# Hybrid encoder layer on one core: side work moved one step apart from what it feeds, and the bias rows made first

## The chip, the cores and the metric

The kernel runs on one core of a Trainium2 chip. The metric is the device time of one execution in microseconds (us), and lower is better. A run here is one timed execution; the kernel before was run three times. One further execution was recorded by the hardware profiler, and all rows below are from that one.

The engines are named as in the profile: PE is the matrix engine (PEld its weight loads), DVE the vector engine, ACT the scalar engine, POOL the general engine, SP the engine that issues most transfers. Each engine works through its own instructions strictly in order, and so does each queue of transfers.

## The reference, cut to what matters

```python
def trunk(x, p, ...):                          # the same weights for 512 + 256 tokens
    proj = rmsnorm(x, norm_g) @ w_in            # 2048 -> 12288
    s_x, s_z, q, k, v, a_z, g_s, g_a = split(proj)
    y = s5(s_x, forward) + s5(s_x, backward) + d * s_x       # state-space scan, 64 groups of 64 states
    y = gelu(y); y = y * sigmoid(y @ glu_w + glu_b); y_s = (y * silu(s_z)) @ w_branch_s
    for h in range(4):                           # difference attention
        s = q[h, c] @ k[h, c].T / sqrt(128) + bias[h]        # c = 0, 1
        w = softmax(s[0]) - lam * softmax(s[1])
        o[h] = w @ v[h]
    y_a = (rmsnorm(o) * 0.2 * silu(a_z)) @ w_branch_a
    x = x + (sigmoid(g_s) * y_s + sigmoid(g_a) * y_a) @ w_out
    x = x + sigmoid(rmsnorm(x, ple_g) @ ple_gate_w) * (p @ ple_proj_w)
    return rmsnorm(x, final_g)
```

## The kernel before, in words

All 768 tokens are held together, features on partitions (128 at a time). The large products with the weights are the main line of the program. Each float32 weight is split into a rounded part (`wh`, made by ACT) and a rest (`wl`, made by DVE), and each product is done as three products of 128x128 by 384 columns. A list of blocks is worked through in order; a block has pieces of 1024 weight columns, and a piece has four products of 12 matmuls. A `Quad` block (it forms q, k and the gates) has seven such products, and DVE and ACT form sums and splits of weights for the next Quad between them.

Everything else runs in lanes beside the main line. A lane is a Python generator. Before a product of the main line, `slot_e` lets each lane write its work for DVE, ACT, POOL and SP up to its next `yield`; after the product, `slot_p` lets it write its work for PE. Two yields are one step. `pace` sets how many steps there are to a product (0.7 early on, `PACE[0..2]` in the state-space part, 0.9 and 1.0 in the attention). So a lane decides by its yields how many products of the main line lie between two of its pieces of work, and if the work that PE needs in a step is not ready when PE comes to it, PE stands still, the main line too.

Four lanes matter here.

- `s5_params` loads the parameters of the state-space part and a one-hot table (`p_oh`, `p_rb`), computes powers of the complex decay (`p_pw`) by a long row of small DVE instructions, and has ACT copy them into tables `tw` and `tq`. After that it makes the four bias rows of the attention: for each head two matmuls into two banks (`bb`), two ACT copies to `bo`, one transfer to `d_bias`. Heads 0 and 2 use banks 4 and 5, heads 1 and 3 banks 6 and 7.
- `s5_half`, run for two halves of the groups, ends with a loop over 8 batches `b`: ACT and DVE copy states into `sb`, SP loads a table `tp` (8 transfers), inputs `u` and a table `q`, and PE forms `yps` from them; ACT copies `yps` to `Y` one turn later, and every second turn 8 transfers write `Y` to `d_yr`. A turn is two steps.
- `att_prep(h)` loads v, k and q of a head from memory (`d_v`, `d_k`, `d_qq`) into one buffer `raw`, scales them and splits each into two parts. The next head's preparation starts before a head is done.
- `att_head(h)` works on six query blocks, one every four steps. `plan_e` and `plan_p` say in which step of a block each function runs: `scores` (PE), `soft1` (DVE: adds the bias, maximum), `expo` (ACT), `soft2` (DVE: the difference of the two softmaxes, in `p`), `wt_pe` (PE: transposes `p` into bank 6, `wt`), `wt_split` (ACT, DVE), `pv` (PE: `o`), `osq`, `ors`, `ors2`, `ocopy` (square, POOL power, scale), `ot_pe` (PE: `ot`, bank 4, which `scores` uses too), `ot_out` (ACT).

The blocks of the gated unit (`ev_glu`: sigmoids on ACT) follow the last Quad. Their inputs `y` are loaded and split (`y_load`, `y_split`) in the last two products of that Quad.

Of the kernel before, what the change touches and what calls it, by code (L numbers as in the profile page):

```python
# [18 lines left out]
EPS = 1e-6  # L19
G = 64  # L20
FB = 11
PACE = 0.9, 0.85, 1.0
IDLE, MPS, ID2 = 5, 2, 2
CONSTS = (("ident", 128), ("norm_g", 16), ("mask16", 16), ("ssm_d", 8), ("final_g", 16), ("glu_b", 8), ("subg", 2),
          ("ple_g", 16), ("lamv", 4))
# [31 lines left out]
def _build(tc, nc, d, es, dbg):  # L57
# [37 lines left out]
    def bank(i, name):  # L95
        return ps.tile([128, 512], F32, tag=f"b{i}", name=name)
# [15 lines left out]
    def later(fn, n=1):  # L112
        pend.append((slot[0] + n, fn))
# [611 lines left out]
    def s5_params(sp):  # L725
# [15 lines left out]
        yield  # L741
        yield

        def dve_exp(out, x):
            xc, n, r, p, m = (t_(k + out.tensor.name) for k in ("xc", "en", "er", "ep", "em"))
            ts(xc, x, -87.0, 88.0, ALU.max, ALU.min)
            ts(n, xc, 1.4426950408889634, 12582912.0, M, A_)
            ts(n, n, -12582912.0, None, A_)
            stt(r, n, -0.693359375, xc, M, A_)
            stt(r, n, 2.12194440e-4, r, M, A_)  # L750
            cs = [1.9875691500e-4, 1.3981999507e-3, 8.3334519073e-3, 4.1665795894e-2,
                  1.6666665459e-1, 5.0000001201e-1]
            ts(p, r, cs[0], cs[1], M, A_)
            for c in cs[2:]:
                tt(p, p, r, M)
                ts(p, p, c, None, A_)
            tt(p, p, r, M)
            tt(p, p, r, M)
            tt(p, p, r, A_)
            ts(p, p, 1.0, None, A_)  # L760
            ts(n, n, 12582912.0 + 127.0, None, A_)
            e = t_("ee" + out.tensor.name, F, I32)
            nc.vector.tensor_scalar(out=e, in0=n.bitcast(I32), scalar1=23, scalar2=None, op0=ALU.logical_shift_left)
            tt(out, p, e.bitcast(F32), M)
            ts(m, x, -87.0, None, ALU.is_ge)
            tt(out, out, m, M)
# [86 lines left out]
        s5c.update(kr=kr, ki=ki, a8r=a8r, a8i=a8i, tw=tw, tq=tq)  # L853
        yield
        yield

        for h in range(4):
            bb = [bank(4, "bb"), bank(5, "bb")] if h % 2 == 0 else [bank(6, "bb"), bank(7, "bb")]
            yield
            for i in range(2):  # L860
                mm(bb[i], rb[:, h], oh[:, i * 512:(i + 1) * 512], True, True)
            yield
            o = pp.tile([128, 1024], F32, tag="bo", name="bo", bufs=2)
            for i in range(2):
                act(o[:, i * 512:(i + 1) * 512], bb[i])
            later(lambda h=h, o=o: dma(dbias[h], o))
        yield
        yield
        yield
# [3 lines left out]
    def s5_half(hf, sp):  # L873
# [205 lines left out]
        for m in range(1, 64):  # L1079
            if m < 32:  # L1080
                S2 = St.rearrange("p (q m) x g -> p q m x g", q=3)[:, 0:3:2]
                prev, cur = S2[:, :, m - 1], S2[:, :, m]
                sh = [128, 2, 2, 32]
                t1 = op.tile(sh, F32, tag="s1", name="s1")
                t2 = op.tile(sh, F32, tag="s2", name="s2")
                tt(t1, prev, a8r.unsqueeze(1).to_broadcast(sh), M)
                tt(t2, prev[:, :, ::-1], a8i.unsqueeze(1).to_broadcast(sh), M)
                f = lambda a: a.rearrange("p q x g -> p q (x g)")
                tt(f(t1), f(t1), f(cur), A_)
                tt(f(cur), f(t1), f(t2), A_)  # L1090
            else:
                prev, cur = St[:, m - 1], St[:, m]
                sh = [128, 2, 32]
                t1 = op.tile(sh, F32, tag="s1", name="s1")
                t2 = op.tile(sh, F32, tag="s2", name="s2")
                tt(t1, prev, a8r, M)
                tt(t2, prev[:, ::-1], a8i, M)
                tt(t1, t1, cur, A_)
                tt(cur, t1, t2, A_)
            if m % 2 == 0:  # L1100
                if m == 44:
                    load_t(0)
                    load_u(0)
                if m == 48:
                    load_q(0)
                if m == 52:
                    load_q(1)
                yield
                yield
# [6 lines left out]
        for b in range(NB + 1):  # L1116
# [11 lines left out]
            if b < NB:  # L1128
# [5 lines left out]
                        act(sb[0:64, :, x, c0:c0 + n], v[0:64])  # L1134
                        nc.vector.tensor_copy(out=sb[64:128, :, x, c0:c0 + n], in_=v[64:128, :, ::-1])
                load_t(b + 1)
                load_u(b + 1)
            yield
            if b < NB:

# [10 lines left out]
                                mm(o, q[:, j - 1, g], sb[:, g, j - 1], False, j == 2)  # L1151
                prevy = (b, yps)
                load_q(b + 2)
            yield
            yield
            yield
        yield
        yield
# [118 lines left out]
    def att_prep(h):  # L1277
# [22 lines left out]
        for n, src, to in (("k", dk, kk), ("q", dqq, qq)):  # L1300
            rw = atile("raw", (128, 2, T), F32)
            for c in range(2):
                dma(rw[:, c], src[(2 * h + c) * 128:(2 * h + c + 1) * 128, :])
            yield
            yield
            yield
            yield
            for c in range(2):
                if n == "q":
                    stt(rw[:, c], rw[:, c], 128.0 ** -0.5, R, M, M)  # L1310
# [15 lines left out]
    def att_head(h, tb, vh, vl, kk, qq):  # L1326
# [98 lines left out]
            later(lambda: dma(dst, ot))  # L1425


        plan_e = {0: soft1, 1: expo, 2: soft2, 3: wt_split, 5: osq, 6: ors, 7: ors2, 8: ocopy, 10: ot_out}
        plan_p = {-1: scores, 2: wt_pe, 4: pv, 9: ot_pe}
        for m in range(-1, 4 * NT + 8):  # L1430
            if m == 4 * NT - 2 and h < 3:
                lane2.add(att_prep(h + 1))
            for plan in (plan_e, plan_p):
                for k in sorted(plan, reverse=True):
                    if (m - k) % 4 == 0 and 0 <= (m - k) // 4 < NT:
                        plan[k]((m - k) // 4)
                yield
# [529 lines left out]
```

## Time and profile before

| | us |
|---|---|
| median of 3 runs | 2511.86 (2506.81 to 2514.24) |
| the profiled execution | 2505.9 |
| its span, first to last instruction | 2504.1 |
| PE busy in the span | 2396.3 (96%) |
| DVE, ACT, POOL busy | 1385.2, 974.1, 149.8 |

The span leaves 1.8 us of the profiled execution outside. A matmul counts as busy until its last column has left the array, and the next has begun by then, so PE's busy time is little more than a statement that PE has work. The time when it is not busy is 108 us, and a part of the busy time is at the lower of PE's two clocks (1.2 GHz in place of 2.4).

### The profile page before, as it was taken

What the parts mean: (1) busy time and instruction counts of PE and PEld (TensorE: products, weight loads), DVE (VectorE), ACT (ScalarE), POOL (GpSimd) and SP (SyncE); (2) the same over time, 40 slices, a digit from 0 to 9 for tenths busy, and PEclk for the clock granted to TensorE, in tenths of its full rate; (3) what the DMA queues carried; (4) which work ended last, traced back from release to release, by engine and by line L of the source; (5) the groups of instructions that cost most, each with busy time, mean ns of one, the idle gap of its engine ahead of it and who ended that gap; (6) DMA issues with size and microseconds to landing.
All of it is one profiled execution on the core that took longest, in us unless ns stands there. A gap on an engine that the chain in (4) does not pass through costs nothing.

```text
span 2504.1 us, 36458 instructions
## 1 busy us (share of the span) xinstructions
PE 2396.3 (96%) x14398; PEld 2354.9 (94%) x14398; DVE 1385.2 (55%) x2569; ACT 974.1 (39%) x1718; POOL 149.8 (6%) x150
## 2 busy tenths in 40 slices
PE   7899999999989999999999899899999999999996
PEld 7799998999989999999898888899999999999986
DVE  8556672566616777654656566557365322253346
ACT  5323213342235555453455555643233211143233
POOL 5000000000000000000111111000000000000003
PEclk9999999999999999999999999999999999999998
DMA  7343235332455677565756557544333222222234
GB/s 293 92 122 116 92 109 165 117 124 100 130 160 152 208 236 210 163 217 133 178 126 149 137 126 176 156 156 164 118 104 112 86 91 78 93 85 87 85 113 163
DMA packets 146347, 345.62 MB, mean 138 GB/s; under 512 B 33600, under 2 KB 55872, under 8 KB 146176
## 3 DMA queue, kind: packets, MB, share of 16 engines
q1 hardware_dynamic: 132352, 306.06, 37.5%
q0 software_dynamic: 13248, 36.18, 9.1%
q8 instruction: 113, 1.85, 0.3%
q10 hardware_dynamic: 576, 1.05, 0.1%
q14 instruction: 58, 0.48, 0.1%
HBM read 238.96 MB, written 104.27 MB: 137 GB/s over the span
## 4 chain that ended last, share of the span: by engine, by line
PE 60%; DVE 3%; ACT 3%; DMA 3%; issue 2%; POOL 1%; SPq 0%; ACTq 0%; DVEq 0%; POOLq 0%
PE acc L93 57%; PE o L93 1%; PE s L93 1%; ACT wh L79 1%; DVE wl L82 1%; POOL y L1649 1%; DMA raw<-d_k 1%; DMA d_az<-stg 1%; PE wt L1379 0%; SPq L99 0%; DVE a L82 0%; DVE p L90 0%; ACT a L79 0%; ACT stg L79 0%; ACT L79 0%
## 5 line engine op out<-in xcount | busy, mean ns | idle before, releaser
L93 PE MATMUL acc<-a,wh 128*128 128x384 f32 (+2 forms) x6072 | 1355.5, 337 | 7.8 <-ACT stg L79 6.2
L93 PEld LDWEIGHTS acc<-a,wh 128*128 128x128 f32 x6072 | 1087.8, 190 | 15.0 <-ACT stg L79 6.5
L93 PE MATMUL acc<-a,wl 128*128 128x384 f32 (+2 forms) x3288 | 878.7, 340 | 16.0 <-DVE wl L82 6.5
L82 DVE TENSOR_TENSOR wl<-raw,wh 128x1024 fp32r<-128x1024 f32 (+1 forms) x279 | 344.9, 1236 | 523.3 <-ACT wh L79 515.2
L93 PEld LDWEIGHTS acc<-a,wl 128*128 128x128 f32 x3288 | 597.4, 190 | 25.8 <-DVE wl L82 6.7
L79 ACT ACTIVATE wh<-raw 128x1024 fp32r<-128x1024 f32 (+1 forms) x321 | 319.6, 996 | 398.9 <-PE acc L93 283.7
L79 ACT ACTIVATE stg<-acc 128x384 f32<-128x384 f32 x312 | 149.2, 489 | 341.0 <-PE acc L93 311.6
L93 PE MATMUL acc<-y,wh 128*128 128x384 f32 (+2 forms) x1024 | 221.8, 335 | 0.0
L93 PEld LDWEIGHTS acc<-y,wh 128*128 128x128 f32 x1024 | 181.0, 188 | 1.8
L93 PE MATMUL acc<-wh,a 128*128 128x256 f32 x768 | 140.3, 285 | 0.0
L93 PE MATMUL acc<-y,wl 128*128 128x384 f32 (+2 forms) x512 | 133.6, 336 | 0.0
L93 PEld LDWEIGHTS acc<-wh,a 128*128 128x128 f32 x768 | 120.9, 194 | 0.0
L93 PE MATMUL acc<-wl,a 128*128 128x256 f32 x384 | 110.6, 288 | 1.8 <-DVE stg L86 1.8
L79 ACT ACTIVATE stg<-stg 128x768 f32<-128x768 f32 (+3 forms) x64 | 43.2, 686 | 173.1 <-DVE stg L82 173.1
L93 PE MATMUL acc<-a,wa 128*128 128x384 f32 x504 | 94.7, 335 | 1.0 <-ACT stg L79 1.0
L79 ACT ACTIVATE stg<-y 128x384 f32<-128x384 f32 (+2 forms) x64 | 32.0, 526 | 160.2 <-DVE y L82 160.2
L93 PEld LDWEIGHTS acc<-y,wl 128*128 128x128 f32 x512 | 92.9, 188 | 0.9
L93 PEld LDWEIGHTS acc<-a,wa 128*128 128x128 f32 x504 | 87.6, 188 | 1.5 <-ACT stg L79 1.4
L93 PEld LDWEIGHTS acc<-wl,a 128*128 128x128 f32 x384 | 74.3, 194 | 2.0 <-DVE stg L86 2.0
L82 DVE TENSOR_TENSOR stg<-acc,R 128x384 f32<-128x384 f32 (+2 forms) x48 | 29.4, 660 | 72.2 <-PE acc L93 72.2
L82 DVE TENSOR_TENSOR y<-acc,stg 128x384 f32<-128x384 f32 x32 | 16.3, 552 | 86.8 <-PE acc L93 86.8
L82 DVE TENSOR_TENSOR raw<-raw,raw 128x512 f32<-128x512 f32 x84 | 58.0, 691 | 2.3
(253 smaller groups left out, 2266.3 us busy)
## 6 DMA issues: line engine op xcount, KB each, us to landing
raw<-in_w_in SPq DMA_DIRECT2D x144, 512.0 KB, 4.2
raw<-in_ple_g_w SPq DMA_DIRECT2D x42, 512.0 KB, 3.6
raw<-in_w_out SPq DMA_DIRECT2D x32, 512.0 KB, 3.6
d_gs<-stg POOLq DMA_DIRECT2D x28, 384.0 KB, 5.9
d_ga<-stg POOLq DMA_DIRECT2D x28, 384.0 KB, 5.4
stg<-in_xT SPq DMA_DIRECT2D x26, 384.0 KB, 4.2
d_q<-q SPq DMA_DIRECT2D x16, 512.0 KB, 3.6
raw<-in_w_v SPq DMA_DIRECT2D x16, 512.0 KB, 4.1
```

The source lines that it names most:

```text
L79: return nc.scalar.activation(out=out, in_=in_, func=func, **kw)
L82: return nc.vector.tensor_tensor(out=out, in0=a, in1=b, op=op)
L93: return nc.tensor.matmul(out, lhsT, rhs, start=start, stop=stop, **kw)
L1649: (nc.gpsimd if b % 3 else nc.vector).tensor_tensor(out=h, in0=h, in1=rb, op=M)
```

## The change

Six edits, all of them in lanes; the main line is the same, product for product.

1. The loop that makes the bias rows stands at the beginning of `s5_params`, before the row of DVE instructions, and no longer after the tables.
2. In the last loop of `s5_half` the two yields that stood behind the products stand between the copies of the states and the products. The turn is still two steps.
3. In the same loop the inputs `u` are loaded two batches ahead and no longer one; `u(1)` is loaded before the loop.
4. In `att_prep` there are six yields between the load of k (and of q) and its first use, where there were four.
5. In `plan_e` and `plan_p` everything from `wt_pe` on is one step later, so that there is one more step between `soft2` and `wt_pe`. The next head's preparation starts one step later.
6. `PACE[1]`, for the scan, is 0.82 and no longer 0.85.

```diff
-PACE = 0.9, 0.85, 1.0
+PACE = 0.9, 0.82, 1.0
...
         yield
         yield
 
+
+        for h in range(4):
+            bb = [bank(4, "bb"), bank(5, "bb")] if h % 2 == 0 else [bank(6, "bb"), bank(7, "bb")]
+            yield
+            for i in range(2):
+                mm(bb[i], rb[:, h], oh[:, i * 512:(i + 1) * 512], True, True)
+            yield
+            o = pp.tile([128, 1024], F32, tag="bo", name="bo", bufs=2)
+            for i in range(2):
+                act(o[:, i * 512:(i + 1) * 512], bb[i])
+            later(lambda h=h, o=o: dma(dbias[h], o))
         def dve_exp(out, x):
...
         s5c.update(kr=kr, ki=ki, a8r=a8r, a8i=a8i, tw=tw, tq=tq)
         yield
         yield
-
-        for h in range(4):
...
-            later(lambda h=h, o=o: dma(dbias[h], o))
         yield
...
                 if m == 44:
                     load_t(0)
                     load_u(0)
+                    load_u(1)
...
                 load_t(b + 1)
-                load_u(b + 1)
+                load_u(b + 2)
+            yield
+            yield
             yield
             if b < NB:
...
                 load_q(b + 2)
             yield
-            yield
-            yield
         yield
...
-            yield
-            yield
-            yield
-            yield
+            for _ in range(6):
+                yield
             for c in range(2):
                 if n == "q":
...
-        plan_e = {0: soft1, 1: expo, 2: soft2, 3: wt_split, 5: osq, 6: ors, 7: ors2, 8: ocopy, 10: ot_out}
-        plan_p = {-1: scores, 2: wt_pe, 4: pv, 9: ot_pe}
+        plan_e = {0: soft1, 1: expo, 2: soft2, 4: wt_split, 6: osq, 7: ors, 8: ors2, 9: ocopy, 11: ot_out}
+        plan_p = {-1: scores, 3: wt_pe, 5: pv, 10: ot_pe}
         for m in range(-1, 4 * NT + 8):
-            if m == 4 * NT - 2 and h < 3:
+            if m == 4 * NT - 1 and h < 3:
                 lane2.add(att_prep(h + 1))
```

Three places show what this does to the order on the engines. The first is ACT near the beginning, in `s5_params`. Before, the copies `bo` of the bias rows stand behind the copies `tw` and `tq` of the tables (`p_sn` and `p_hs` are sines, `wh` the splits of the main line's weights):

```order
L79 ACTIVATE wh_872<-raw_641 128x1024
L79 ACT_TABLE_LOAD
L79 ACTIVATE p_sn<-p_r 128x64
L79 ACTIVATE p_hs<-p_rh 128x64
L79 ACTIVATE wh_992<-raw_724 128x1024
L79 ACTIVATE tw<-p_pw 64x512 x2
L79 ACTIVATE tq<-p_pw 64x512 x2
L79 ACTIVATE tw<-p_pw 64x512 x2
L79 ACTIVATE tq<-p_pw 64x512 x2
L79 ACTIVATE wh_1096<-raw_870 128x1024
L79 ACTIVATE bo<-bb 128x512 x6
L79 ACTIVATE wh_1178<-raw_990 128x1024
```

After the change the same stretch of ACT, from the split of the same piece of weights (`raw_641`) on, is this:

```order
L79 ACTIVATE bo<-bb 128x512 x2
L79 ACTIVATE wh_819<-raw_641 128x1024
L79 ACTIVATE bo<-bb 128x512 x6
L79 ACTIVATE wh_932<-raw_724 128x1024
L79 ACT_TABLE_LOAD
L79 ACTIVATE p_sn<-p_r 128x64
L79 ACTIVATE p_hs<-p_rh 128x64
L79 ACTIVATE wh_1068<-raw_817 128x1024
L79 ACTIVATE tw<-p_pw 64x512 x2
L79 ACTIVATE tq<-p_pw 64x512 x2
L79 ACTIVATE tw<-p_pw 64x512 x2
L79 ACTIVATE tq<-p_pw 64x512 x2
```

The bias copies have moved ahead of the sines and tables, and the tables one piece of weights (four products) further back.

The second place is SP in the last loop of `s5_half`, one turn and the beginning of the next. Before:

```order
L99 DMA tp<-d_z 16x4x128 x8
L99 DMA u<-d_sx 128x384
L99 DMA q<-d_q 128x1024
L99 DMA d_yr<-y 16x8x96 x8
L99 DMA tp<-d_z 16x4x128 x8
```

After:

```order
L99 DMA tp<-d_z 16x4x128 x8
L99 DMA u<-d_sx 128x384
L99 DMA d_yr<-y 16x8x96 x8
L99 DMA q<-d_q 128x1024
L99 DMA tp<-d_z 16x4x128 x8
```

The `u` there is now that of one batch later, and the 8 writes of `Y` stand before the load of `q`, which waits for the products of the turn.

The third place is DVE in a query block of the second head: `soft2` (`r`, `s`, `p`), and the next block of rows up to `wtl`, which needs PE's transposes of that `p`. Before:

```order
L1370 RECIPROCAL r<-su 128x2
L90 SCALAR_TENSOR_TENSOR s_13284<-r,nlam,su 128x1
L90 SCALAR_TENSOR_TENSOR p<-p,s_13284 128x512
L82 TENSOR_TENSOR wl<-raw_13126,wh 128x1024
L82 TENSOR_TENSOR ors<-ors,r 128x1
L82 TENSOR_TENSOR wtl<-wt,wth 128x512
```

After:

```order
L1369 RECIPROCAL r<-su 128x2
L90 SCALAR_TENSOR_TENSOR s_13371<-r,nlam,su 128x1
L90 SCALAR_TENSOR_TENSOR p<-p,s_13371 128x512
L82 TENSOR_TENSOR wa<-raw_13259,wa 128x512
L82 TENSOR_TENSOR raw_13259<-raw_13259 128x512
L87 TENSOR_SCALAR rsm<-oss 128x1
L82 TENSOR_TENSOR raw_13259<-raw_13259,raw_13152 128x512
L82 TENSOR_TENSOR raw_13152<-raw_13152,raw_13259 128x512
L82 TENSOR_TENSOR ors<-ors,r 128x1
L82 TENSOR_TENSOR wtl<-wt,wth 128x512
```

One more product's worth of the main line's splits and sums lies between the difference and what follows its transposes.

Two more facts of the order. The lane of the attention ends 14 products of the main line later than before, so that the last head lies wholly beside the blocks of the gated unit, whose sigmoids need another function table on ACT than the exponentials; ACT has 18 table loads in place of 12. And the last head's q (2 transfers) now stands on SP right before the 8 loads of `y`.

## Rows read from the trace of the kernel before

**Rows 1.** The page: span, and busy time, share and instructions of PE.

```profile
span 2504.1 us, 36458 instructions
PE 2396.3 (96%) x14398; PEld 2354.9 (94%) x14398; DVE 1385.2 (55%) x2569; ACT 974.1 (39%) x1718; POOL 149.8 (6%) x150
```

**Rows 2.** Windows: start:end, length, each engine's busy time (instructions), granted clock, DMA share, GB/s.

```profile
375.00:445.00 70.00, 64.19 (x463) 62.78 (x462) 19.15 (x52) 25.18 (x58) 0.00 (x0) 1.00 0.56 160
665.00:742.00 77.00, 68.63 (x456) 67.06 (x456) 20.09 (x63) 26.02 (x61) 0.00 (x0) 1.00 0.56 159
1190.00:1600.00 410.00, 367.94 (x2100) 356.63 (x2099) 248.39 (x460) 216.01 (x443) 64.62 (x80) 0.95 0.65 150
```

**Rows 3.** Waits of PE, whole span: what waited, releaser, us in total, times, longest.

```profile
PE wt L1379 <- DVE p L90: 26.8, 16, 7.4
PE acc L93 <- ACT stg L79: 11.3, 5, 6.2
PE bb L93 <- ACT bo L79: 7.7, 1, 7.7
...
PE yps L93 <- DVE sb L1135: 4.1, 5, 1.4
...
PE yps L93 <- DMA u<-d_sx: 3.4, 3, 2.0
PE s L93 <- DVE ql L82: 2.9, 1, 2.9
```

**Rows 4.** Timeline, tables and bias rows: start, us, instruction [idle before, releaser].

```profile
105.85 2.25 ACT L79 ACTIVATE tw<-p_pw 64x512 f32<-64x512 f32 x2 [13.83 <-DVE p_pw L82]
...
114.57 1.06 ACT L79 ACTIVATE wh<-raw 128x1024 fp32r<-128x1024 f32 x1
...
116.17 3.77 PE L93 MATMUL bb<-p_oh,p_rb 32*128 32x512 f32 x4 [7.66 <-ACT bo L79]
```

**Rows 5.** Windows on the stretches at half clock: the first; the sum of seven in attention.

```profile
113.18:123.42 10.24, 7.25 (x15) 4.71 (x16) 1.23 (x1) 5.55 (x9) 0.00 (x0) 0.50 0.55 205
...
sum 37.54, PE 29.23 PEld 28.88 DVE 24.75 ACT 16.47 POOL 5.24; mean PE 4.18 PEld 4.13 DVE 3.54 ACT 2.35 POOL 0.75
```

**Rows 6.** Timeline, two turns of the last state-space loop.

```profile
384.64 0.55 ACT L79 ACTIVATE y<-yps 128x192 f32<-128x192 f32 x2 [2.89 <-PE yps L93]
385.09 1.85 ACT L79 ACTIVATE sb<-st 64x256 f32<-64x256 f32 x4
385.24 3.71 SPq L99 DMA_DIRECT2D tp<-d_z  x8
...
397.90 1.10 PE L93 MATMUL yps<-sb,q 128*128 128x96 f32 x8 [1.40 <-DVE sb L1135]
```

**Rows 7.** Timeline, one query block of the second head.

```profile
1385.69 0.47 ACT L79 ACTIVATE on<-o,r 128x256 f32<-128x256 f32 x1 [0.94 <-PE o L93]
...
1391.80 0.63 PE L1379 MATMUL wt<-consts,p 128*128 128x128 f32 x4 [1.73 <-DVE p L90]
```

**Rows 8.** Timeline, preparation of the third head.

```profile
1433.36 1.91 DVE L82 TENSOR_TENSOR raw<-raw,R 128x768 f32<-128x768 f32 x2 [4.66 <-DMA raw<-d_k]
...
1441.72 4.21 PE L93 MATMUL acc<-a,wh 128*128 128x384 f32 x12 [6.22 <-ACT stg L79]
```

**Rows 9.** Timeline, end of the last Quad and loads of `y`.

```profile
1577.92 2.25 PE L93 MATMUL acc<-a,wl 128*128 128x384 f32 x12
1584.39 0.84 ACT L79 ACTIVATE a<-a 128x768 fp32r<-128x768 f32 x1 [1.93 <-DMA a<-d_y]
...
1587.55 1.08 PE L1379 MATMUL wt<-consts,p 128*128 128x128 f32 x4 [7.38 <-DVE p L90]
```

**Rows 10.** Timeline, transposed output `ot` and its copy, second head.

```profile
1387.58 0.38 PE L1418 MATMUL ot<-consts,on 128*128 128x128 f32 x2
1389.11 0.62 ACT L79 ACTIVATE ot<-ot,subg 128x128 f32<-128x128 f32 x2
```

**Rows 11.** Groups of ACT: table loads, count, busy us, mean ns of one, idle before.

```profile
L79 ACT ACT_TABLE_LOAD x12 | 15.4, 1283 | 2.2 <-issue 1.3 <-PEq L1957 0.7
```

More of the change, by code (lines that the diff above doesn't have):

```diff
@@ L855, in s5_params @@
         yield
-        for h in range(4):
-            bb = [bank(4, "bb"), bank(5, "bb")] if h % 2 == 0 else [bank(6, "bb"), bank(7, "bb")]
-            yield
-            for i in range(2):
-                mm(bb[i], rb[:, h], oh[:, i * 512:(i + 1) * 512], True, True)
-            yield
-            o = pp.tile([128, 1024], F32, tag="bo", name="bo", bufs=2)
-            for i in range(2):
-                act(o[:, i * 512:(i + 1) * 512], bb[i])
-            later(lambda h=h, o=o: dma(dbias[h], o))
         yield
@@ L1303, in att_prep @@
                 dma(rw[:, c], src[(2 * h + c) * 128:(2 * h + c + 1) * 128, :])
-            yield
-            yield
-            yield
-            yield
+            for _ in range(6):
+                yield
             for c in range(2):
```

## Prediction

> **What bounds the kernel now.** I read the page first. PE is busy for 2396.3 of 2504.1 us [rows 1]: the main line fills the span, and lanes cost time only where PE stands still for them, or where they cost it its clock. What can be won is therefore in PE's idle 108 us and in the stretches at half clock, and a lane's own length costs nothing as long as some of the main line is left beside it. Next I read the waits of PE over the whole span [rows 3]. The largest by far is the transposes' wait for `soft2` on DVE: 26.8 us in 16 pieces, the longest 7.4. Then come the main line's wait for an ACT copy (11.3), the bias rows' wait for ACT (7.7, one piece), several kinds of wait before the `yps` products, and one wait of the first scores (2.9). Windows show where they lie [rows 2]. In the two last loops of the state-space part PE is idle for 70.00 - 64.19 = 5.8 and 77.00 - 68.63 = 8.4 us, 14.2 together. In the 410 us of attention beside the Quads it is idle for 42 us, and the granted clock is 0.95. DVE is busy there for 248 and ACT for 216 of 410 us, so neither is short of time; what PE waits for is lateness in single steps. Last I looked at the stretches at half clock one by one [rows 5]. All seven of the attention's follow on a standstill of PE. In them PE is busy for 29.23 us, work that takes 14.6 us at full clock: 14.6 us lost on top of the idle time.
>
> A step of the lanes is worth one product of the main line where the pace is 1.0. Twelve matmuls show 2.25 us, the last one's tail included [rows 9]; 2.1 us is what I use.
>
> **Bias rows first.** Before, the third bias group needs banks 4 and 5 emptied by `bo`, and these copies stand behind the tables: ACT waits 13.83 us for DVE's powers, then copies from 105.85 to 114.57, 8.7 us, and only then comes to a split and to `bo` [rows 4]. PE loses 7.66 us and after it runs 7.25 us at half clock, another 3.6 [rows 5]. After the change the groups wait for nothing: the one-hot table has been loaded two steps earlier, and ACT has no long wait ahead of `bo`. The late thing is now the tables. They move back by four steps, at pace 0.7 some 3.0 us each, 12 us, and by up to 16 if DVE, now without its powers to do, first waits for the evacuation of a block. So ACT's 8.7 us end between 126.6 and 130.6, and the split behind them (1.06, and about as much again for its rest on DVE) is ready between 129 and 133. PE, without its standstill, is back from the bias group at 108.5 and has two such groups (4 us before or after) and nine products (19 us) to do until it needs that split, at 131. I take a wait of 2 us that takes the place of 7.7, and half of the slow clock: 5.7 + 1.8 = 7.5 us won. Bounds: nothing (a new wait as long as the old one), and 11.3.
>
> **The last loop of the state-space part.** Copies and products had one product of the main line between them, now they have two. The copies cannot start earlier than before in one respect: ACT's `y` copies, which stand ahead, wait for the products of the turn before, and these now lie in the step just before. From there ACT needs 0.55 + 1.85 = 2.4 us [rows 6] against 4.2, and with a split of 1.06, every second turn, 3.5; that is covered. DVE's copies were late by 1.4 behind a split [rows 6]; one more product covers that. `u` loaded two ahead ends the waits for it (3.4). SP needs 3.71 us for `tp` [rows 6], about as much for the writes of `Y` every second turn, and two single transfers, some 6.4 a turn; PE's turn is 4.2 plus 24 small products, which at the row's 1.10 for eight make 3.3 at most. SP just keeps up, and `tp` keeps its four steps. I let 2 of the 14.2 us stand: 12.2 won. Bounds: 3.4 (only `u`), and 14.2. The pace 0.82 puts a little more than one product more beside each scan, at no cost, since the main line goes on for long after.
>
> **The step after `soft2`.** Without the longest, 15 waits make 19.4 us, 1.3 each; 1.73 is one of them [rows 7]. A step of 2.1 us covers nearly all; 1 us stays. In addition `expo` stood behind the square `on` on ACT, which waits for PE's `o` (0.94 there [rows 7]); that square now runs one step after `expo`, which makes the chain shorter. The longest wait, 7.38 us, is another thing: `soft2` stood on DVE behind the splits of `y`, and ACT's fourth split waited for its transfer until 1584.39 [rows 9]. PE was through with the Quad at about 1580 and needs these very splits next. So the transposes no longer wait there, but the gated unit's first product does. With the last head's q now ahead of `y` on SP, this may even last longer. I leave 5 us. Won: 26.8 - 1 - 5 = 20.8. Bounds: 13 (7.4 stays and a third of the rest returns), and 25.
>
> **Loads of k and q.** DVE stood 4.66 us for k's transfer, and PE 6.22 us in consequence, through ACT's copy of a product's bank [rows 8]. One more step takes 2.1 from that and leaves 4.1; the other main-line waits of the kind (the rest of 11.3, all but half a us) and the scores' 2.9 shrink to some 0.8 together. Won: 14.2 - 4.9, about 9. Bounds: 4 and 13. The later end of the attention costs nothing: its lane is followed by one that has some 28 steps' worth of main line left and needs 24.
>
> **Clock.** Fewer and shorter standstills give back part of the 14.6 us; I keep 6 for those left at `y` and at one preparation: 8.6 won. Bounds: 3 and 12.
>
> **What is added.** The copy of `ot` out of bank 4 now has one product, not two, before `scores` wants the bank. In the tightest block the transposes end at 1387.96 and the copy at 1389.73 [rows 10], where one product more ends at 1389.9: 0.2 us to spare. I charge 2 us over the 12 places. Six more table loads are 6 x 1.28 = 7.7 us of ACT [rows 11]. They lie before `expo`, which has the new step as cover, and before the sigmoids, which two free pairs of banks cover; so nothing on PE's path. Without that cover they cost 7.7. The Trainium skill, ScalarE: Activation LUTs, section "What ACT_TABLE_LOAD costs", counts a drain with each load, about 2.66 us a switch, and its rules say to do all of one set before switching, which speaks against moving the whole last head beside sigmoids. By it the six would be 16 us of ACT. The trace shows 1283 ns a load and only 2.2 us idle ahead of all twelve [rows 11], so the trace's price is the one used. Last, a wait that goes lets the next late thing show. For that I charge a quarter of the step's and the loads' gain, 7.5 us.
>
> **Sum.** 7.5 + 12.2 + 20.8 + 9 + 8.6 = 58.1, less 2 and 7.5: 48.6. The profiled execution was 2505.9, so 2457.3. The three runs lie 0.9 to 8.3 us above that execution; I add 3 and forecast **2460 us**.
>
> **Rivals.**
> *Half of it returns.* In attention PE goes faster and DVE and ACT must keep up; three quarters of the 38.4 us (step, loads, clock) come back as waits of the main line for splits and bank copies. For it: these queues are in order, and one late landing moves everything behind it [rows 8]. Against it: both engines are idle for 40% of that stretch [rows 2]. 7.5 + 12.2 + 9.6 - 2 = 27.3, with the 3 added 2482. Chance 0.18.
> *ACT paces the last head.* All six table loads fall on PE's path: 7.7 more, 2468. For it: `expo` and the sigmoids alternate four steps apart. Against it: the cover above. Chance 0.08. [...]
> *The change does not do what it says.* Each wait moves one step along with what was moved: the tables hold up the main line for 7 us, `y` copies hold back `sb` by a us in each of 16 turns, the attention's waits return in full. 2500 to 2512, chance 0.07. Against it: two of the three need the engines to be full.
> *Slower.* `scores` behind `ot`: where ACT is late, PE waits in the 12 places in which the bank is wanted one step later. It decides from 48.6/12 = 4 us of lateness each; at 5 us it is 60 lost, 2520. For it: a spare of 0.2 us [rows 10], and ACT was once over 6 us late [rows 8]. Against it: that was one transfer in 410 us. Chance 0.05.
>
> **Chances and range.** The forecast has 0.62, with 2445 to 2472 as its own range. Low end: nothing of the 9.5 us charged comes, and a few us of what I left standing go too. The high end of the whole reaches past the first rival, to 2490; outside lie the last two rivals and a little on the low side. About 0.3%, 7.5 us, is what a measurement of this kernel can tell from no change. Faster by more than that: 0.62 + 0.18 + 0.08 = 0.88; within: 0.07; slower: 0.05.
>
> **What would show it.** Right: no wait of `bb` for `bo`; PE's waits before `yps` under 4 us together; `wt` waits for `soft2` under 3 us; a wait of the main line of about 5 us for splits of `y` at the end of the last Quad; a smaller one at one preparation; half-clock stretches in attention under half of 37.5 us; 18 table loads of 1.28 us. The forecast is wrong if PE waits for `ot`, if waits of `acc` for ACT or DVE grow by more than 15 us, or if the split behind the tables holds PE for 5 us or more.

## The result and the profile after

The changed kernel takes 2445.70 us, median of 4 runs (2443.91 to 2450.41), beside 2509.34 (2506.47 to 2514.24, 4 runs) for the kernel before: a ratio of 0.9747, 95% interval 0.9725 to 0.9770, a gain of 63.6 us. The forecast was 2460 us with 2445 to 2490 as its range: the sign and the places were right, the gain was 15 us larger than the sum of 48.6, and the time lies 0.7 us above the low end of the range. The profiled execution is the shortest of the four and has a span of 2442.2 us; its granted clock, as a share of the full 2.4 GHz over the whole span, was 0.992, and the four had 0.992, 0.989, 0.990 and 0.992. The kernel before had 0.985 in its profiled execution.

The page of the changed kernel, which answers to [rows 1]:

```profile
span 2442.2 us, 36464 instructions
PE 2379.0 (97%) x14398; PEld 2341.8 (96%) x14398; DVE 1384.6 (57%) x2569; ACT 980.0 (40%) x1724; POOL 151.9 (6%) x150
```

PE does the same 14398 matmuls. It is idle for 2442.2 - 2379.0 = 63.2 us, where it was 107.8: 44.6 of the 61.9 us of span. Another 17.3 us went from its busy time. Stretches at half clock account for most of them: PE was busy in these for 53.8 us before and is for 23.1 us now, and half of the difference, 15.4 us, is time won. The sums of all windows at half clock, before and after:

```profile
sum 78.75, PE 53.85 PEld 50.94 DVE 44.43 ACT 28.67 POOL 12.25; mean PE 3.85 PEld 3.64 DVE 3.17 ACT 2.05 POOL 0.88
```

```profile
sum 40.18, PE 23.07 PEld 21.10 DVE 25.36 ACT 17.56 POOL 9.73; mean PE 3.85 PEld 3.52 DVE 4.23 ACT 2.93 POOL 1.62
```

PE's waits in the changed kernel, whole span (what waited, releaser, us in total, times, longest), against [rows 3]:

```profile
PE wt L1378 <- DVE p L90: 6.5, 1, 6.5
PE acc L93 <- ACT a L79: 5.5, 5, 2.2
PE acc L93 <- ACT stg L79: 5.1, 6, 1.6
PE yps L93 <- DMA tp<-d_z: 2.8, 2, 1.4
...
PE yps L93 <- DMA d_yr<-y: 1.9, 1, 1.9
...
PE o L93 <- ACT on L79: 0.6, 1, 0.6
PE yps L93 <- issue: 0.6, 1, 0.6
```

The 16 waits of `wt` (26.8 us) have become one. The waits of `bb` for `bo` and of `s` for `ql` have no row any more, and those before `yps` are down to 2.8 + 1.9 + 0.6 = 5.3 us, but for another cause: SP's queue and the landing of `tp`.

Windows of the changed kernel over the same parts of the program (start:end, length, busy time of each engine, granted clock, DMA share, GB/s), against [rows 2]:

```profile
375.00:445.00 70.00, 65.40 (x445) 64.20 (x445) 18.18 (x45) 24.96 (x58) 0.00 (x0) 1.00 0.64 181
665.00:742.00 77.00, 75.61 (x505) 75.19 (x505) 19.98 (x47) 33.94 (x72) 0.00 (x0) 1.00 0.66 202
1180.00:1580.00 400.00, 385.67 (x2259) 375.14 (x2258) 259.00 (x485) 234.71 (x474) 65.55 (x80) 0.98 0.68 163
```

In the attention beside the Quads PE stands still for 14 of 400 us where it was 42 of 410. All of the half clock left there lies in two stretches, at the end of the last Quad, with 8.77 + 3.37 = 12.14 us of PE's work:

```profile
1513.11:1523.35 10.24, 8.77 (x25) 7.27 (x26) 7.15 (x8) 7.02 (x10) 0.86 (x1) 0.50 1.04 359
1540.42:1547.25 6.83, 3.37 (x10) 2.90 (x11) 3.95 (x11) 6.09 (x11) 0.00 (x0) 0.50 0.32 91
```

What happens there, and the one wait that is left of the tables, in the timeline of the changed kernel (start, us, engine, what, idle before and its releaser; rows of five engines):

```profile
135.31 0.59 PE L93 MATMUL acc<-a,wl 128*128 128x384 f32 x2 [1.83 <-DVE wl L82]
...
1503.83 0.80 SPq L99 DMA_DIRECT2D raw<-d_qq  x2
1506.16 6.39 SPq L99 DMA_DIRECT2D a<-d_y  x8
...
1512.05 0.84 ACT L79 ACTIVATE a<-a 128x768 fp32r<-128x768 f32 x1 [4.44 <-DMA a<-d_y]
1512.94 0.88 PE L93 MATMUL acc<-a,wl 128*128 128x384 f32 x2 [2.17 <-ACT a L79]
...
1519.64 0.86 POOL L325 DMA_DIRECT2D d_ga<-stg  x1 [11.77 <-ACT stg L79]
1525.31 1.78 POOL L325 DMA_DIRECT2D d_ga<-stg  x2 [4.81 <-DMA d_ga<-stg]
1532.68 1.28 ACT L79 ACT_TABLE_LOAD   x1 [7.73 <-DMA d_ga<-stg]
1535.73 1.03 DVE L82 TENSOR_TENSOR stg<-stg 128x384 f32<-128x384 f32 x2 [7.80 <-DMA stg<-d_ysz]
1539.44 0.68 DVE L1349 CUSTOM_DVE_ANT_0 p<-s,tb 128x512 f32<-128x512 f32 x1
1543.88 1.09 PE L1378 MATMUL wt<-consts,p 128*128 128x128 f32 x4 [6.46 <-DVE p L90]
```

The last head's q and the eight tiles `y` leave SP together, so ACT waits for `y` and PE for ACT. ACT's copy of the Quad's last banks stands behind, and so do the Quad's last stores on POOL, which add to what is in memory and go one after the other. The gated unit's first sigmoid, and the load of `d_ysz` that it is multiplied with, come only after these have landed, by the releaser that the rows give. DVE works in order, so `soft1` stands behind that product, and the transposes wait for `soft2`.

### The profile page after: what moved, and what is told of

It is laid out like the page before. It is cut to its first block, busy times and chain, and to the rows that moved or that the text cites. A ratio compares the mean times of both kernels' runs of the same rounds, so it can differ in the third digit from the quotient of the medians.

```text
span 2442.2 us, 36464 instructions
## 1 busy us (share of the span) xinstructions
PE 2379.0 (97%) x14398; PEld 2341.8 (96%) x14398; DVE 1384.6 (57%) x2569; ACT 980.0 (40%) x1724; POOL 151.9 (6%) x150
## 4 chain that ended last, share of the span: by engine, by line
PE 87%; DMA 4%; DVE 4%; ACT 2%; issue 2%; POOL 1%; SPq 1%; POOLq 0%; ACTq 0%; DVEq 0%
PE acc L93 79%; PE yps L93 2%; PE vps L93 1%; PE o L93 1%; PE s L93 1%; PE kps L93 1%; DVE a L90 1%; DVE a L82 1%; ACT a L79 1%; DVE wl L82 1%; POOL y L1648 1%; DMA d_ga<-stg 1%; PE wps L1046 1%; ACT wh L79 1%; SPq L99 1%
```

## The experiments

All times below are medians with the ratio to the kernel before on the same chip (in brackets its 95% interval). The changed kernel stands at 2445.7 and 0.9747. The runs come from several chips, so a difference of medians and a difference of ratios are two estimates of the same thing; they lie up to 4 us apart here, and both are given where it matters.

### Each edit undone alone

**Edit 5 undone**, the step after `soft2`:

```diff
-        plan_e = {... 2: soft2, 4: wt_split, 6: osq, ...}; plan_p = {-1: scores, 3: wt_pe, 5: pv, 10: ot_pe}
+        plan_e = {... 2: soft2, 3: wt_split, 5: osq, ...}; plan_p = {-1: scores, 2: wt_pe, 4: pv, 9: ot_pe}
-            if m == 4 * NT - 1 and h < 3:
+            if m == 4 * NT - 2 and h < 3:
```

> Edit 5 undone alone (everything from the transposes on one step earlier again, next preparation one step earlier). Theory, each edit pays at its own place: PE's waits of wt for DVE's p come back to 20 to 27 us in about 16 pieces and the clock of the attention loses 6 to 8 us again, so 22 to 30 us slower than the changed kernel. Rival, the edits in the attention stand in for one another (the later loads and uses of edit 4 already spread DVE's work): under 14 us slower.

Measured: 2471.88 us, ratio 0.9839 (0.9819 to 0.9860), 26.2 us slower by the medians and 23.1 by the ratios. The first theory holds for the waits and not for the clock. A row of its waits and a window over the attention up to the last loads of `y`:

```profile
PE wt L1378 <- DVE p L90: 21.9, 18, 2.3
```

```profile
1180.00:1530.00 350.00, 323.87 (x1913) 312.32 (x1912) 221.83 (x412) 192.68 (x399) 60.34 (x74) 1.00 0.67 152
```

PE stands still for 26 of these 350 us, in pieces of at most 2.3, and the granted clock is 1.00 all the time. So here the short waits for `soft2` cost their own length and no clock. That they never do is not shown: in the kernel before, one of the same length was followed by half clock. First a wait of this run, then the one of the kernel before, with the window behind it:

```profile
1241.35 0.63 PE L1378 MATMUL wt<-consts,p 128*128 128x128 f32 x4 [1.98 <-DVE p L90]
```

```profile
1474.26 0.63 PE L1379 MATMUL wt<-consts,p 128*128 128x128 f32 x4 [1.98 <-DVE p L90]
```

```profile
1475.10:1478.51 3.41, 3.41 (x12) 3.41 (x11) 1.29 (x2) 0.52 (x2) 0.00 (x0) 0.50 0.91 204
```

**Edit 1 undone**, the bias rows behind the tables again (the loop over `bb` moves back below `s5c.update`).

> Edit 1 undone alone (bias rows behind the tables again). Theory: the wait of bb for bo of 7.7 us returns in place of the wait of 1.8 us behind the tables, with its stretch at half clock (3.6 us): 9 us slower, 7 to 11. Rival, PE's time at the beginning is made up later since the lanes behind it start as they did: under 4 us slower.

Measured: 2455.77 us, 0.9776 (0.9756 to 0.9795), 10.1 slower by the medians, 7.3 by the ratios: the theory. The old wait is back, and its slow stretch (timeline; window):

```profile
116.51 3.77 PE L93 MATMUL bb<-p_oh,p_rb 32*128 32x512 f32 x4 [7.68 <-ACT bo L79]
```

```profile
111.22:124.87 13.65, 8.36 (x19) 5.82 (x20) 1.96 (x3) 8.25 (x12) 0.00 (x0) 0.50 0.41 154
```

**Edits 2 and 3 undone**, the last state-space loop:

```diff
-                    load_u(1)
...
-                load_u(b + 2)
-            yield
-            yield
+                load_u(b + 1)
...
             yield
+            yield
+            yield
```

> Edits 2 and 3 undone together (products one step after the copies again, u loaded one batch ahead). Theory: the waits before yps return from 5 to about 14 us, so 9 us slower, 7 to 11. Rival, part of the gain read at the two loops came from edit 6 or from the clock: under 5 us slower.

Measured: 2456.05 us, 0.9775 (0.9755 to 0.9796), 10.4 slower by the medians, 7.0 by the ratios. The size is that of the theory, the way is not. Waits and stretches at half clock in the two loops:

```profile
PE yps L93 <- issue: 4.8, 3, 2.3
PE yps L93 <- DMA d_yr<-y: 1.8, 1, 1.8
PE yps L93 <- DMA u<-d_sx: 0.6, 1, 0.6
PE yps L93 <- PE acc L93: 0.6, 1, 0.6
```

```profile
sum 10.24, PE 10.14 PEld 10.17 DVE 3.18 ACT 1.68 POOL 0.00; mean PE 5.07 PEld 5.09 DVE 1.59 ACT 0.84 POOL 0.00
```

The waits rise from 5.3 to 7.8 only, not to the 14 of before, and PE runs 10.14 us at half clock in the loops (5.1 us lost), where neither the kernel before nor the changed one loses clock ([rows 2] and the windows above: 1.00). That this clock belongs to the two edits is not shown: of the eleven traces that have both edits, eight have a stretch of 3.41 to 6.83 us at half clock in the first of these loops too, behind the wait for `d_yr`. The two edits were not run apart.

**Edit 4 undone**, four yields between a load of k or q and its use:

```diff
-            for _ in range(6):
-                yield
+            yield
+            yield
+            yield
+            yield
```

> Edit 4 undone alone (four yields between a load of k or q and its first use). Theory: the main line's waits for ACT's bank copies go from 5 back to about 11 us, the scores' wait of 2.9 returns, and some 2 us of clock: 9 to 12 us slower. Rival, one of edits 4 and 5 is enough for these waits, since edit 5 also starts the preparation a step later: under 5 us slower.

Measured: 2458.26 us, 0.9790 (0.9770 to 0.9810), 12.6 slower by the medians, 10.8 by the ratios: the theory, or a little more. Waits, and the sum of the four stretches at half clock in the attention:

```profile
PE acc L93 <- ACT stg L79: 13.9, 7, 6.1
...
PE s L93 <- DVE ql L82: 2.9, 1, 2.9
```

```profile
sum 20.47, PE 17.44 PEld 17.15 DVE 14.18 ACT 8.83 POOL 4.99; mean PE 4.36 PEld 4.29 DVE 3.55 ACT 2.21 POOL 1.25
```

The long waits are back (the 6.1 lies at 1311, the preparation of a head), and with them the half clock in the middle of the attention: three of the four stretches follow on waits of the preparations (2.88, 6.09 and 3.65 us). This ties the clock to the preparations; that the step has no part in it is not shown (see the wait of 1.98 us above).

**Edit 6 undone**, the pace of the scan:

```diff
-PACE = 0.9, 0.82, 1.0
+PACE = 0.9, 0.85, 1.0
```

> Edit 6 undone alone (0.85 for the scan). Theory, the pace only moves the scan's steps by a little more than one product and costs and gives nothing: within 3 us of the changed kernel (2442 to 2449). Rival, the four single undoings (59 us together, of 64) leave 4 to 5 us that belong to the pace: 4 us or more slower.

Measured: 2456.47 us, 0.9773 (0.9752 to 0.9794), 10.8 slower by the medians, 6.5 by the ratios, whose intervals overlap; its shortest run (2450.80) is above the longest of the changed kernel, but the kernel before was 3.3 us slower beside it too. By both estimates it is the rival and not my theory, though the ratios alone do not decide. Waits before `yps`, and of the four stretches at half clock from 300 to 750 the first and the sum (the changed kernel has none there):

```profile
PE yps L93 <- DMA tp<-d_z: 6.0, 3, 2.8
...
PE yps L93 <- DMA d_yr<-y: 3.6, 1, 3.6
```

```profile
311.32:314.73 3.41, 3.41 (x19) 3.41 (x18) 3.24 (x13) 0.00 (x0) 0.00 (x0) 0.50 0.94 320
...
sum 17.06, PE 16.16 PEld 16.19 DVE 3.54 ACT 3.57 POOL 0.00; mean PE 4.04 PEld 4.05 DVE 0.89 ACT 0.89 POOL 0.00
```

The waits before `yps` are 9.6 us in place of 5.3, and a wait of 1.77 us of the main line for a DVE evacuation beside the scan is back at 310, which the kernel before had at 317 and the changed kernel does not have. Four of these five waits are followed by half clock: 16.16 / 2 = 8.1 us lost. The wait beside the scan and its stretch belong to the pace: all three traces with 0.85 have both (this one, the kernel before and the run of edit 5 alone below), and none of the eleven with 0.82. The stretch near 430 comes in most traces with 0.82 as well. That the pace shifts the loops against the pieces of the main line, so that other loads and stores meet on SP, is my reading; no run tests it.

The five undoings make 26.2 + 10.1 + 10.4 + 12.6 + 10.8 = 70.1 us by the medians and 23.1 + 7.3 + 7.0 + 10.8 + 6.5 = 54.7 by the ratios, against 63.6 for the whole: the edits add up to within what these runs can tell. Whether some of them share a gain is not shown.

How much clock an edit gives back cannot be read from one trace. The wait behind the tables lasts 1.82 to 1.87 us in all eleven traces with edit 1. In nine of them it is followed by half clock, as here with the pace undone, and in two, of which the changed kernel's is one, it is not:

```profile
133.46 0.66 PE L93 MATMUL acc<-a,wl 128*128 128x384 f32 x2 [1.85 <-DVE wl L82]
```

```profile
133.82:137.24 3.42, 3.42 (x13) 3.42 (x12) 3.42 (x7) 0.13 (x1) 0.00 (x0) 0.50 0.76 231
```

The mean granted clock over the four or five runs of a kernel is steadier. It is 0.991 for the changed kernel, 0.989 with edit 1, with edits 2 and 3 and with edit 4 undone, 0.990 with edit 6 undone, and 0.991 with edit 5 undone. So undoing edit 5 costs no clock over the runs either, and each of the others some 2 to 4 us. The runs of each of these kernels differ by up to 0.003 among themselves, so this is a sign and no more.

### Edit 5 alone

> The kernel before with edit 5 alone (everything from the transposes on one step later, next preparation one step later). Theory, the edits add up: about 26 us faster than before, 20 to 30, with PE's waits of wt for DVE's p down to one or two, the preparations' waits for ACT's bank copies (about 11 us) and for ql still there, and most of the stretches at half clock in the attention still there too, since those come with the long waits for the preparations. Rival: the step carries the whole gain in the attention, clock included, 35 us or more.

Measured: 2479.75 us, 0.9879 (0.9865 to 0.9892), 30.2 us faster than 2509.96 beside it: just past the top end of the theory. What is left is what the theory said, the long waits and their clock (waits; sum of the four stretches at half clock in the attention, of which PE had 29.23 us before [rows 5]):

```profile
PE acc L93 <- ACT stg L79: 14.7, 7, 6.2
...
PE s L93 <- DVE ql L82: 3.6, 1, 3.6
```

```profile
sum 20.48, PE 15.08 PEld 14.31 DVE 14.21 ACT 7.98 POOL 4.43; mean PE 3.77 PEld 3.58 DVE 3.55 ACT 1.99 POOL 1.11
```

In these two traces the attention has 29.23 - 15.08 = 14.2 us less at half rate, 7.1 us; two of the stretches that have gone followed on waits for `soft2`, of 2.94 us at 1247 and of 1.98 at 1474. Over all runs the step alone wins hardly any clock: 0.986 here, 0.985 in the nine runs of the kernel before beside it. So what it gives back in clock stays open, and is small.

### The end of the last Quad

Six runs tried to remove the two standstills that are there now (3.5 us before the main line, 6.5 before `wt`).

Four yields for the last head only, `for _ in range(6 if h < 3 else 4)`:

> The changed kernel with four yields in place of six in the preparation of the last head alone, so that its q is loaded earlier and its use lies elsewhere than the loads and splits of y. Theory, the new standstills at the end of the last Quad (3.5 us before the main line and 6.5 before wt, with 6 us of clock) come from y standing behind q on SP: 6 to 12 us faster than the changed kernel (about 2436). Rival, they come from the stage buffers that are taken anew there, which wait for the Quad's last stores whatever q does: within 3 us of the changed kernel.

Measured: 2449.69 us, 0.9750 (0.9735 to 0.9765), no gain. The two waits grew to 6.83 and 8.46 us. The run does not test its theory, for the edit did not part q from `y`: q leaves SP at 1510.78 and `y` at 1513.74, where it was 1503.83 and 1506.16.

The first four tiles of `y` earlier (the diff is shortened; they also go to other space and are split in place):

```diff
-    hooks[j - 2, 5] = [y_load]
+    hooks[j - 2, 1] = [lambda: y_load(range(4))]
+    hooks[j - 2, 5] = [lambda: y_load(range(4, 8))]
...
```

> The changed kernel with the first four tiles of y loaded four products earlier, into space that the last Quad has done with after its first product, and split in place; the other four are loaded where they were. Theory, one late thing starts a chain: y is late, ACT's copy of the Quad's last bank stands behind its splits, the Quad's last stores go out late, and the gated unit's first stage buffer and then soft1 and soft2 wait for these. Then both standstills go: 8 to 14 us faster than the changed kernel (about 2434). Rival, two separate causes: the waits before the main line go (3.5 us and 2 to 3 of clock), the 6.5 us before wt stay: 4 to 6 us faster.

Measured: 2442.84 us, 0.9733 (0.9719 to 0.9746): 2.9 less than the changed kernel, which the intervals do not tell from none. The waits are 2.96 us before the main line and 4.77 before `wt`: both shrank, and neither theory's form came. The second half of `y` now left SP at 1508.49, later than the whole had.

> Both of these: four yields for the last preparation, and y in two loads. If y is the one late thing and either cure is enough: as the better of the two alone, within 3 us. If they cure different waits: the two gains add up, 12 us or more faster than the changed kernel.

Measured: 2446.66 us, 0.9747 (0.9733 to 0.9760): the gains did not add up, and it is 3.8 us above the better of the two, which the intervals do not tell from none; the waits are 5.37 and 7.38 us. The second half of `y` again stands right behind q on SP.

k and q loaded with v, straight into the tiles of their rests (the diff is shortened; the loads that stood behind are gone):

```diff
+        kl, ql = [[atile(f"{n}l{c}") for c in range(2)] for n in "kq"]
+        for lo, src in ((kl, dk), (ql, dqq)):
+            for c in range(2):
+                dma(lo[c].bitcast(F32), src[(2 * h + c) * 128:(2 * h + c + 1) * 128, :])
...
```

> The changed kernel with k and q of a head loaded at the start of its preparation, with v, straight into the tiles that later hold their rests (kl, ql), so that no load of q stands near the loads of y; all yields as in the changed kernel. Theory, the loads of y at the end of the last Quad are late because q's 786 KB and y's 3.1 MB come together: the 3.5 us before the main line and the 6.5 before wt shrink to half, 5 to 10 us faster than the changed kernel. Rival, the 16 transfer engines are full there with the Quad's accumulating stores and the weights anyway: within 3 us.

Measured: 2443.17 us, 0.9723 (0.9703 to 0.9744): 2.5 us faster by the medians, which is the rival, and 6.0 by the ratios, which is the theory; the intervals overlap, so the time decides nothing and the trace has to. Transfers at the end of the Quad (KB each, median us from issue to landing), first the changed kernel, then this one:

```profile
a<-d_y SPq DMA_DIRECT2D x8, 384.0 KB, 8.8
```

```profile
a<-d_y SPq DMA_DIRECT2D x8, 384.0 KB, 6.1
```

With q out of the way a tile of `y` takes 2.7 us less from issue to landing, which fits that q delayed it, and PE's wait for it falls from 3.5 to 1.95 us; the wait before `wt` does not change (6.8). So what shortens the first standstill does not touch the second: they have two causes.

The same with shorter preparations (against the run before):

```diff
-            for _ in range(6):
+            for _ in range(2):
                 yield
```

> The same with two yields in place of six between a head's preparation steps for k and q, so that each head starts four products earlier and the last head lies earlier against the end of the last Quad by some sixteen. Since the loads left 6 yields and more ahead, no wait for them should return: theory, what stands still at the end of the last Quad depends on which piece of the last head meets the loads of y, and with the head's preparation done before them both waits go: 8 to 16 us faster than the changed kernel. Rival, y is late by the filling of the transfer engines whatever else lies there, and the wait before wt becomes one before another product: within 4 us.

Measured: 2439.84 us, 0.9711 (0.9691 to 0.9732), the shortest median of all, 5.9 below the changed kernel by the medians and 9.0 by the ratios, with intervals that still overlap: between the rival's 4 and the theory's 8 to 16. The wait before `wt` is gone; as the rival had it, two others stand in its place (timeline):

```profile
1527.91 0.79 PE L93 MATMUL s<-kl,qh 128*128 128x512 f32 x1 [4.22 <-ACT ot L79]
...
1549.76 0.38 PE L93 MATMUL o<-vl,wth 128*128 128x256 f32 x1 [3.39 <-ACT on L79]
```

The first is the rival "slower" of the prediction, `scores` behind ACT's copy out of `ot`, at the 4 us each from which it would have decided, but at one place and not at twelve.

Last, the stage buffers turned, on top of `h1_inplace`:

```diff
+    for _ in range(2):
+        nc.vector.memset(stg()[:, 0:1], 0.0)
```

> As h1_inplace (k and q loaded early, all yields as in the changed kernel), with the ring of five stage buffers turned by two at the start (two buffers are taken there with a memset of one column each), so that the last Quad's three tiles lie in buffers 2 to 4, and the three stage buffers that are taken anew for the gated unit lie on 0 to 2, of which only the third still waits for those last stores. Theory, the 6.8 us before wt in h1_inplace (6.5 in the changed kernel) come from the gated unit's first sigmoid waiting for the Quad's last stores to leave that memory, with soft1, expo and soft2 queued behind it: the wait goes, or shrinks under 2 us, ACT's wait for d_ga at its first table load goes, and with the clock the time falls by 6 to 9 us against h1_inplace, to about 2435. Rival, soft1 is late there by DVE's splits of y and the table loads: the wait before wt keeps more than 4 us, and the time stays within 3 us of h1_inplace.

Measured: 2445.61 us, 0.9744 (0.9725 to 0.9763), 2.4 us above `h1_inplace`: the theory fell in the form I gave it, and the wait before `wt` stays at 6.74 us, as the rival forecast. Timeline:

```profile
1533.64 1.28 ACT L79 ACT_TABLE_LOAD   x1 [7.84 <-DMA d_ga<-stg]
```

ACT still waits for the last stores, though by my layout the first two new buffers no longer lie on them; where they do lie no trace shows. Whether the wait is for single buffers, for the whole pool as it is opened anew, or for something else that the stores hold, stays open. The rival's own cause, DVE busy with splits of `y`, is not in the row: what ACT waits for is `d_ga`. Apart from the kernel before, PE waits more than 4.7 us for `soft2` before `wt` in nine traces, and all nine share that ACT's first table load for the gated unit is released by `d_ga`, after 3.0 to 8.2 us of standing still; but the two lengths do not go together (8.46 of PE behind 3.48 of ACT in the first run of these six), so the chain is not shown to be the whole cause.

## Why the prediction was right, and where its sum was off

*What bounds the kernel.* Right: the gain came from PE's standstills (44.6 us) and from its clock (15.4), with nothing taken from the main line. Two of the signs named for being right did not come: the waits before `yps` are 5.3 us (under 4 was named), and those of `wt` 6.5 (under 3).

*Bias rows first.* 7.5 forecast; in the trace 7.66 - 1.83 = 5.8 us of idle time and 3.6 of clock, 9.4, and 10.1 when undone. The wait of 2 us behind the tables came as 1.83. It was followed by no slow stretch, where I had charged half of one; this is luck of the traced execution, since in nine of eleven traces the same wait is followed by a stretch of 3.41 us at half clock, 1.7 us lost.

*The last loop of the state-space part.* 12.2 forecast, 14.2 - 5.3 = 8.9 measured. The step that failed is "SP just keeps up": what is late now is `tp` and the stores of `Y` on SP. A second step failed beside it: the pace "at no cost" is worth 6.5 us by the ratios and 10.8 by the medians, in these loops and at 310.

*The step after `soft2`.* 20.8 forecast. `wt` gives back 26.8 - 6.5 = 20.3, and the new 3.5 us before `y` come off: 16.8. The 1 us left over the short waits was too much, none is left. The 5 us left at `y` were 10, since the transposes wait there too, which I had ruled out. I had seen that q stands ahead of `y` and named it; the chain through the stores I had not.

*Loads of k and q.* 9 forecast, 9.1 measured: 11.3 - 5.1 and 2.9; the undoing gave 12.6 with its clock. The size agrees in part by luck. A wait of 4.1 us was to stay at one preparation and 0.8 us of all the rest; what stays is six waits of 1.6 us at most, 5.1 together. DVE waits for the third head's k less than 0.8 us at a time, where it was 4.66, so the step covers more than it was charged with.

*Clock.* 8.6 forecast for the attention, 14.6 - 6.1 = 8.5 measured. That the sizes agree is in part luck: the 6 us kept were for `y` and one preparation, and all that is left is at the end of the Quad. The first reason given, that all seven stretches follow on a standstill, is true and too coarse: 18 standstills of up to 2.3 us cost no clock when edit 5 was undone, one of 1.98 did in the kernel before, and the long ones of the preparations did when edit 4 was undone. What I didn't count is outside the attention: two stretches, at 318 and 1130, have gone and one came at the start, 1.7 us net, and the one I expected behind the tables did not come, 1.8. The one at 1130 is no gain of the edits: eight of the other traces with a change have one between 1109 and 1143. Another 1.5 us came back at the end of the program.

*What is added.* The 9.5 us charged did not come, and this is the largest term of the miss. PE never waits for `ot`, and `o` behind `on` fell to 0.6 us from this row of before; the square now runs behind `expo`, which is the likely reason (with edit 5 alone it is 2.1, one wait of 1.5 at the end among them):

```profile
PE o L93 <- ACT on L79: 3.7, 4, 1.9
```

Six more table loads are there. Beside the gated unit, from 1547 to 1680, PE has one wait of over 0.3 us, of 0.59, so they cost next to nothing on its path:

```profile
L79 ACT ACT_TABLE_LOAD x18 | 23.1, 1283 | 8.8 <-DMA d_ga<-stg 7.7 <-PEq L1956 0.7
```

Of 8.8 us idle ahead of 18 loads, 7.7 are the one wait for stores. Where ACT waits for nothing else, 0.02 us lie ahead of a load and 0.01 behind it. By the drain that the Trainium skill counts with each load (ScalarE: Activation LUTs, "What ACT_TABLE_LOAD costs"), these 18 would take some 48 us of ACT, an estimate from its 2.66 us a switch; the trace has 23.1, with 1.1 us idle ahead of the other 17, so here the load's own 1.28 us is the whole price, and the measurement decides.

*The sum.* 9.4 + 8.9 + 16.8 + 9.1 + 8.5 + 3.1 (`o`) = 55.8 of the 61.9 us of span; other clock 3.3, other waits 0.9, and 1.9 us of tails and matmul records that I don't place.

*The rivals.* "Half of it returns" is out: main-line waits for ACT's bank copies fell. "ACT paces the last head" is out by the row above. "The change does not do what it says" is out: every undoing is slower, by both estimates. "Slower" did not occur, and its mechanism showed once, in a variant.

## What to carry to other kernels

A step inserted between a late producer and an in-order PE pays the sum of the short waits that it covers, and its price elsewhere can be small if the other engines are idle for 40% of that stretch; charge for it only what a row shows. Count long waits and short ones apart: in these traces every standstill of over 4 us once PE has begun is followed by half clock, and one of about 2 us is in some executions and not in others, so compare the clock over several runs and not in one trace. A change of pace that looks free moves a lane's transfers against the main line's: undo it alone before calling it nothing.

## What the runs showed of the hardware

The transfer engines are full at the end of the last Quad at very different rates. Windows of the changed kernel (the last two columns are the share of 16 engines and GB/s; a transfer counts where it begins, so a share can come out above 1):

```profile
1510.00:1515.00 5.00, 2.71 (x10) 1.89 (x9) 0.96 (x1) 0.84 (x1) 0.00 (x0) 0.81 1.04 251
1515.00:1520.00 5.00, 3.65 (x10) 2.65 (x10) 3.03 (x4) 3.67 (x6) 0.36 (x1) 0.50 1.03 412
```

Busy to the same share they move 251 or 412 GB/s. From 1495 to 1540 POOL's queue, whose transfers there are the stores that add, moves 2.36 MB in 30.8% of the engines' time, and SP's 8.56 MB in 54.3%: 13 against 6.3% for a MB. So by their times `y`'s 3.1 MB wait for more than their own bytes. Whether it is the adding that costs is not shown: no run has these stores without it.

A standstill's length alone does not tell whether the clock falls: 1.77 us at 310 with the pace undone was followed by 3.41 us at half clock, and 2.33 us with edit 5 undone, at 1445, by none. One and the same wait, 1.82 to 1.87 us behind the tables, was followed by half clock in nine traces and not in two.
